# A hybrid convolution and attention block: sums of token quarters split where they are formed

## The chip, the cores and the metric

The kernel runs on one core of a Trainium2 chip. The metric is the time of one execution on the device in microseconds, as the median of several runs. TensorE (PE) does the matmuls, VectorE (DVE), ScalarE (ACT) and GpSimd (POOL) the elementwise work; transfers are issued from the queue of SyncE (SP) and, for some stores, from that of ACT, and run on 16 DMA engines.

## The reference, cut to what matters

A single decoder layer over 2048 tokens of width 1024. All matrices are float32.

```
h = rms_norm(x, norm_w) * (1 + scale) + shift
z = h @ w_in
a, b, g_conv, q, k, v, g_attn, m_conv, m_attn = split(z)
u = silu(layer_norm(causal_conv31(a * sigmoid(b)))) * silu(g_conv)
y_conv = u @ w_conv_out
o = merge of three groups of dilated window attention over rope(rms_norm(q)), rope(rms_norm(k)), v
y_attn = (o * silu(g_attn)) @ w_attn_out
y = sigmoid(m_conv) * y_conv + sigmoid(m_attn) * y_attn
out = x + gate * (y @ w_out)
```

The change concerns `h` on its way into the products with those columns of `w_in` that do not belong to q, k and v.

## The kernel before, in words

**Float32 products out of two parts.** A float32 matrix X is written as an upper part h, X rounded to TensorE's fp32r format, and a lower part l = X - h, also in fp32r. A product takes three matmuls per piece: upper with upper, upper with lower, lower with upper. Making the two parts is called a split here: ACT copies X into h (`nc.scalar.activation(h, raw, AF.Copy)`) and DVE or POOL subtracts (`l = raw - h`). Weights are split as they arrive from memory, activations as they are made.

**First stage: q, k, v and attention.** There are 12 units (three groups of four heads), numbered 0 to 11. A unit goes through 16 steps, one for each block of 128 tokens (`NB`). In a step PE does 24 matmuls of 384 columns (`z_tokens`, L549), and parts of the attention of earlier blocks run between them (`attend_step`), at matmul 5 (flow `beside`) and matmul 14 (flow `main`). After the matmuls ACT and DVE empty the PSUM bank, norm and rotate (`project_step`: squares on ACT L572, their inverse root on POOL L114 and L115, then DVE L586 and L593 to L596). Other small jobs are hung into the steps by `at_step(u, j, m, f)`: f is issued in step j of unit u, before matmul m.

**The matrix h stays in SBUF as quarters.** `hi` and `lo` hold h transposed, in eight tiles each, for half the channels (kh = 0, 1) and 512 tokens (t = 0 to 3). A copy of h in float32 is in memory (`h_d`).

**Second stage: the remaining columns by Strassen's scheme.** The tokens are taken in two halves of 1024. For each half and each pair of 128-column blocks, seven products replace eight (`quad`, L1091). In words of `PRODUCTS`, the left factors are in order A11, A12, S2, S1, S3, S4, A22. Three of them (A11, A12, A22) are quarters of h, the four others are sums and differences of quarters. A product is 12 matmuls of 512 columns. There are 22 jobs (one `quad` each) per half, of kinds `ab_quad` (feeds the convolution), `gate_quad` and `ag_quad`. A slot is one product; slots follow one another in the list `slots`; the last two jobs of the first half and the first two of the second half are interleaved, product by product. Inside a job, ACT copies intermediate sums out of PSUM (`kept`, L1097), DVE adds (L1104, L1118), POOL adds (L1115), and gates are applied on ACT (L1217) and stored. Weights are loaded nine slots ahead (L1039, L1041), combined (L1046) and split seven slots ahead (L1054 on ACT, L1055 on DVE or POOL). DVE runs the convolution in small pieces between all that (`run_conv`), so many per slot.

**How the sums come about before the change.** In units 3 to 7 quarters of h are fetched from `h_d` (`quarter_fetch`, L849) into three tiles of 512 columns, DVE forms the four sums (`quarter_sum`, L853), and each is stored in float32 in `s_d` (L854). This is done eight times (two halves, four channel blocks), 9 steps apart.

**How they land.** *First passage* (from the attention to the first half): in the last unit, whose token blocks are visited in the order 3, 4, ..., 15, 0, 1, 2, the quarters of h that are not needed any more are replaced. From its step 6 on S1, from its step 10 on S2 and S3 are loaded in pieces of 256 columns into a tile `raw`, and one step later ACT and DVE split them into the quarter (`quarter_load` L889, `quarter_split` L895 and L896). S4 is loaded in four pieces of 512 columns into four of the ten buffers of the weights' tile (`wr`) and split in the first four slots. *Second passage* (from the first half to the second): as the interleaved jobs finish product n, its left factor of the first half is given up, and that of the second half is loaded into landing tiles, two pieces per slot, and split two slots later, on ACT and on DVE (for the fourth channel block on POOL). This holds for all seven left factors.

**What sets the order.** The order on PE is the order in the program (`manual_schedule`). On the other engines a planner orders the instructions by a simulated timeline, except for those under `tc.keep_in_program_order`, which keep their place. A queue runs its instructions in order, SP's and ACT's DMA issues among them, and one that waits holds up what is behind it.

The lines that the change and the prediction touch: L849, L853, L854 (forming and storing), L883 to L899 (landing), L902 to L905 (the plan of the first passage), L914 to L925 (the last unit), L1000 and L1001, L1311 to L1325 (S4), L1346 to L1354 (second passage). In the profile the landing tiles are called `rawS`, `s` (S4) and `landingS` or `landingA`; the quarters `S_hi`, `S_lo`, `A_hi`, `A_lo`.

Of the kernel before, what the change touches and what calls it, by code (L numbers as in the profile page):

```python
# [10 lines left out]
F32 = mybir.dt.float32  # L11
F32R = mybir.dt.float32r
# [42 lines left out]
def tile_hybrid_block(  # L55
# [36 lines left out]
    s_d = dram.tile([2, 4, 4, P, 512], F32, name="s_d")  # L92
# [753 lines left out]
    def quarter_fetch(half, k, names):  # L846
        for name, i, kh, t in names:
            q = aside["sq", name] = aside["sq"].tile([P, 512], F32, tag=f"sx{i}", name=f"sx{half}_{k}_{name}")
            nc.sync.dma_start(q, h_d[4 * kh + k, :, 1024 * half + 512 * t : 1024 * half + 512 * t + 512])  # L849

    def quarter_sum(half, k, n, dst, x0, x1, op):
        q = [aside["sq", name] for name in (dst, x0, x1)]
        tc.keep_in_program_order(nc.vector.tensor_tensor(*q, op=op))  # L853
        nc.sync.dma_start(s_d[half, n - 1, k], q[0])  # L854
# [6 lines left out]
    for i in range(8):  # L861
        half, k = divmod(i, 4)
        at = NB * 3 + 8 + 9 * i
        for n, f in ((0, lambda half=half, k=k: quarter_fetch(half, k, (("21", 0, 0, 1), ("22", 1, 1, 1), ("11", 2, 0, 0)))),
                     (1, lambda half=half, k=k: quarter_sum(half, k, 1, "22", "21", "22", ALU.add)),
                     (2, lambda half=half, k=k: quarter_sum(half, k, 3, "21", "11", "21", ALU.subtract)),
                     (4, lambda half=half, k=k: quarter_sum(half, k, 2, "11", "22", "11", ALU.subtract)),
                     (5, lambda half=half, k=k: quarter_fetch(half, k, (("12", 1, 1, 0),))),
                     (7, lambda half=half, k=k: quarter_sum(half, k, 4, "12", "12", "11", ALU.subtract))):
            at_step((at + n) // NB, (at + n) % NB, 23, f)  # L870
# [11 lines left out]
    def quarter_src(half, name, k):  # L882
        if name[0] == "S":  # L883
            return s_d[half, int(name[1]) - 1, k]
        kh, t = {"A11": (0, 0), "A12": (1, 0), "A22": (1, 1)}[name]
        return h_d[4 * kh + k, :, 1024 * half + 512 * t : 1024 * half + 512 * t + 512]
# [4 lines left out]
    def quarter_split(half, name, k, cols, raw, eng):  # L891
# [5 lines left out]
        if half == 0 and name == "S4":  # L897
            tc.keep_in_program_order(i1)
            tc.keep_in_program_order(i2)  # L899
# [870 lines left out]
```

## Time and profile before

| | |
|---|---|
| median of 3 runs | 2373.52 us |
| lowest, highest | 2368.76, 2375.06 us |
| span of the profiled execution | 2368.3 us |
| mean granted clock of TensorE | 0.997 |
| PE busy | 2325.8 us (98%) |
| DVE busy | 1737.0 us (73%) |
| ACT busy | 1020.9 us (43%) |
| POOL busy | 836.1 us (35%) |
| moved by DMA | 378.57 MB, mean 160 GB/s |

The span goes from the first to the last instruction of one profiled execution; the profile does not give that execution's own time beside it. Times on the time axis are microseconds from the start of the span. In a row of the timeline stand start, duration, engine, line of the program, operation, output and inputs, shapes, count, and in brackets the idle time before it and what ended that. In a row of waits stand who waited for whom, the sum, the number and the longest. On the time axis, the attention stage ends near 1076, the second stage begins there, its second half begins near 1513, and the last stages (the projections of both branches, the merge and the output projection) begin near 1930.

### The profile page before, as it was taken

The numbers are of one execution on the slowest core, as the hardware profiler recorded it, in microseconds if no ns is written. First come the engines' busy times: TensorE is split into PE (matmuls) and PEld (weight loads), VectorE is DVE, ScalarE is ACT, GpSimd is POOL, SyncE is SP. The second block draws the span as 40 slices with busy tenths as digits, with TensorE's granted clock in tenths as the row PEclk, the third lists the DMA queues.
The fourth block names the chain that finished last, engine by engine and source line by source line (L and its number), as shares of the span: only waits on it lengthen the run. The fifth ranks groups of instructions, "written<-read, shape, count | busy, mean of one in ns | idle before, by whom it ended". The sixth has DMA issues, their size and how long they took to land.

```text
span 2368.3 us, 38785 instructions
## 1 busy us (share of the span) xinstructions
PE 2325.8 (98%) x12421; PEld 2083.0 (88%) x12421; DVE 1737.0 (73%) x4104; ACT 1020.9 (43%) x2825; POOL 836.1 (35%) x976
## 2 busy tenths in 40 slices
PE   6999999999999999999999999999999999999999
PEld 4899999999999999997888888788888888878887
DVE  7855655555556777776699999989968768787654
ACT  5733343343344555456444444544444444332221
POOL 4321111111111111123677778656556730000221
PEclk9999999999999999999999999999999999999999
DMA  7733544454552222144535445745444569876552
GB/s 279 241 116 117 160 125 144 149 169 149 158 162 67 60 80 67 47 123 154 170 135 176 160 152 195 241 130 151 139 150 134 165 213 330 292 236 204 185 167 102
DMA packets 354121, 378.57 MB, mean 160 GB/s; under 512 B 27688, under 2 KB 249176, under 8 KB 353918
## 3 DMA queue, kind: packets, MB, share of 16 engines
q1 hardware_dynamic: 312622, 314.05, 42.6%
q10 hardware_dynamic: 41296, 62.05, 7.5%
q8 instruction: 99, 1.62, 0.3%
q14 instruction: 104, 0.85, 0.1%
HBM read 235.34 MB, written 140.64 MB: 159 GB/s over the span
## 4 chain that ended last, share of the span: by engine, by line
PE 88%; DMA 4%; DVE 4%; ACT 2%; issue 1%; POOL 1%; SPq 0%; ACTq 0%; DVEq 0%; POOLq 0%
PE pz L549 31%; PE paab L1091 7%; PE yc L1399 6%; PE oa L1681 4%; PE pcab L1091 4%; PE pag_mc_d L1091 4%; PE pag_g_d L1091 3%; PE pag_ma_d L1091 3%; PE po L684 3%; PE ps L635 3%; PE ya L1399 2%; PE pcg_g_d L1091 2%; PE oc L1681 2%; PE pbab L1091 2%; PE paag L1091 2%; PE pcg_mc_d L1091 2%
## 5 line engine op out<-in xcount | busy, mean ns | idle before, releaser
L549 PE MATMUL pz<-wh_u,hT_lo 128*128 128x384 f32 x1504 | 525.2, 349 | 2.5 <-DVE hT_lo L371 2.4
L549 PE MATMUL pz<-wh_u,hT_hi 128*128 128x384 f32 x1504 | 505.6, 336 | 1.3 <-ACT hT_hi L369 1.3
L549 PE MATMUL pz<-wl_u,hT_hi 128*128 128x384 f32 x1504 | 505.8, 336 | 0.0
L114 POOL TENSOR_SCALAR st<-st 128x2 f32<-128x2 f32 x192 | 44.9, 234 | 797.0 <-ACT sq L572 796.7
L586 DVE SCALAR_TENSOR_TENSOR qk<-pz,st,wqk 128x128 f32<-128x128 f32 x384 | 116.9, 346 | 265.0 <-POOL st L115 260.8
L549 PEld LDWEIGHTS pz<-wh_u,hT_lo 128*128 128x128 f32 x1504 | 283.2, 188 | 4.0 <-DVE hT_lo L371 3.7
L549 PEld LDWEIGHTS pz<-wh_u,hT_hi 128*128 128x128 f32 x1504 | 283.8, 189 | 2.2 <-ACT hT_hi L369 1.9
L549 PEld LDWEIGHTS pz<-wl_u,hT_hi 128*128 128x128 f32 x1504 | 282.8, 188 | 0.5 <-issue 0.5
L627 ACT ACTIVATE qkT<-ptq 128x256 f32<-128x256 f32 x192 | 73.8, 384 | 358.1 <-PE ptq L620 302.5
L1169 DVE SCALAR_TENSOR_TENSOR ce<-us,pair_taps,ce 128x512 f32<-128x512 f32 x240 | 180.9, 754 | 6.5
L1140 DVE SCALAR_TENSOR_TENSOR ce<-ut,chan,ce 128x512 f32<-128x512 f32 x240 | 179.8, 749 | 0.0
L1055 POOL TENSOR_TENSOR slT<-wT,shT 128x512 fp32r<-128x512 f32 x107 | 143.8, 1345 | 79.8 <-ACT shT L1054 79.5
L1153 DVE SCALAR_TENSOR_TENSOR cq<-ut,chan,cq 128x512 f32<-128x512 f32 x208 | 156.0, 750 | 1.0
L1054 ACT ACTIVATE shB<-wB 128x512 fp32r<-128x512 f32 x130 | 82.1, 631 | 161.7 <-PE paab L1091 51.7
L115 POOL TENSOR_TENSOR st<-st,mhalf 128x2 f32<-128x2 f32 x192 | 140.1, 729 | 15.9
L572 ACT ACTIVATE sq<-pz 128x128 bf16<-128x128 f32 x384 | 106.1, 276 | 78.7 <-PE pz L549 68.9
L1054 ACT ACTIVATE shT<-wT 128x512 fp32r<-128x512 f32 x110 | 69.4, 631 | 160.9 <-POOL wT L1046 32.0
L1055 POOL TENSOR_TENSOR slB<-wB,shB 128x512 fp32r<-128x512 f32 x85 | 111.9, 1317 | 76.1 <-ACT shB L1054 73.8
L684 PE MATMUL po<-lv,pT 128*128 128x128 f32 x596 | 96.8, 274 | 0.0
L684 PEld LDWEIGHTS po<-lv,pT 128*128 128x128 f32 x596 | 90.9, 190 | 0.6 <-issue 0.5
L593 DVE TENSOR_TENSOR t<-qk,tab 128x256 f32<-128x256 f32 x192 | 82.5, 430 | 5.7
L1055 POOL TENSOR_TENSOR slT<-wB,shT 128x512 fp32r<-128x512 f32 x57 | 75.1, 1324 | 28.4 <-ACT shT L1054 28.3
(783 smaller groups left out, 6163.2 us busy)
## 6 DMA issues: line engine op xcount, KB each, us to landing
wB<-in_w_in_dram SPq DMA_DIRECT2D x154, 256.0 KB, 3.2
qkv_d<-qkv SPq DMA_DIRECT2D x128, 192.0 KB, 2.3
wT<-tT_d SPq DMA_DIRECT2D x88, 256.0 KB, 2.7
tT_d<-wB ACTq DMA_DIRECT2D x66, 256.0 KB, 2.7
lqk<-qkv_d SPq DMA_DIRECT2D x128, 128.0 KB, 2.3
raw_u<-in_w_in_dram SPq DMA_DIRECT2D x84, 192.0 KB, 3.6
acc_d<-osb SPq DMA_DIRECT2D x128, 65.0 KB, 2.0
part<-acc_d ACTq DMA_DIRECT2D x64, 130.0 KB, 2.4
```

Source lines behind the costliest of these rows:

```text
L115: nc.gpsimd.tensor_tensor(dst, scratch[:, :n], mhalf[:, :n], op=ALU.pow)
L549: nc.tensor.matmul(pz[:, :width], part(a, k, P * j, P), w[:, :width], start=(m == 0), stop=(m == 23))
L586: nc.vector.scalar_tensor_tensor(qk[:, 2 * i : 2 * i + 2].rearrange("p a b -> p (a b)"), pz[:, P * i : P * i + P], st[:, 2 + i : 3 + i], w ...
L684: nc.tensor.matmul(po[:, :P], box["pT"][:, P * i : P * i + P], vt, start=(i == 0), stop=(i == nk - 1))
L1054: nc.scalar.activation(h, q[name], AF.Copy)
L1055: eng.tensor_tensor(l, q[name], h.bitcast(F32), op=ALU.subtract)
L1091: nc.tensor.matmul(ps, w, x, start=(m == 0 and ps.name not in first), stop=(m == 11 and not more), skip_group_check=True)
L1140: stt(box["e"], e[:, 1 + j : 513 + j], chan[:, cb, 2 * j : 2 * j + 1], box["e"], op0=ALU.mult, op1=ALU.add)
L1153: stt(box["o"], o[:, 2 + j : 514 + j], w, psum_o, op0=ALU.mult, op1=ALU.add)
L1169: stt(dst, box["both"][:, 1 + j : 513 + j], pair_taps[:, cb, j : j + 1], box["e"], op0=ALU.mult, op1=ALU.subtract if j == 0 else ALU.add)
L1399: nc.tensor.matmul(pz, w, xx, start=(m == 0), stop=(m == len(terms) - 1))
L1681: nc.tensor.matmul(ps, y, w, start=(m == 0 and ps.name not in begun), stop=(m == 11 and not more), skip_group_check=True)
```

## The change

The sums are split where they are formed, and both parts are stored in `s_d`, which becomes twice as large. Forming goes in 16 rounds of 256 columns instead of 8 of 512, 4.5 steps apart instead of 9. In a round four quarters are fetched into four tiles of 256 columns, and from a step and a half later on, at four successive half steps (before matmuls 10 and 23), one sum each is formed: DVE adds, ACT copies the upper part, DVE subtracts for the lower part, all three pinned to the program's order, and SP stores both parts. The parts share three buffers (`sxs`).

At both passages the parts are loaded straight into the quarter's two tiles (`sum_land`), two transfers of 512 columns for each channel block, with no landing tile, copy or subtraction. The load itself now waits until the quarter's old content is done with. The quarters A11, A12 and A22 of the second half land and are split as before. At the first passage S1 is loaded from step 6 of the last unit, S2 and S3 from its step 10, three blocks in two steps; S4 is loaded ahead of the first slots and no longer uses the weights' buffers. At the second passage the loads stand where those of the landing tiles stood.

```
-    s_d = dram.tile([2, 4, 4, P, 512], F32, name="s_d")
+    s_d = dram.tile([2, 2, 4, 4, P, 512], F32, name="s_d")
...
+    def quarter_fetch(half, k, c):
+        for name, kh, t in (("21", 0, 1), ("22", 1, 1), ("11", 0, 0), ("12", 1, 0)):
+            q = aside["sq", name] = aside["sq"].tile([P, 256], F32, tag=f"sx{name}", name=f"sx{half}_{k}_{c}_{name}")
+            t0 = 1024 * half + 512 * t + c
+            nc.sync.dma_start(q, h_d[4 * kh + k, :, t0 : t0 + 256])
+
+    def quarter_sum(half, k, c, n, dst, x0, x1, op):
         q = [aside["sq", name] for name in (dst, x0, x1)]
+        h, l = (aside["sq"].tile([P, 256], F32R, tag="sxs", name=f"sx{hl}{half}_{k}_{c}_{n}", bufs=3) for hl in "hl")
         tc.keep_in_program_order(nc.vector.tensor_tensor(*q, op=op))
-        nc.sync.dma_start(s_d[half, n - 1, k], q[0])
+        tc.keep_in_program_order(nc.scalar.activation(h, q[0], AF.Copy))
+        tc.keep_in_program_order(nc.vector.tensor_tensor(l, q[0], h.bitcast(F32), op=ALU.subtract))
+        for i, x in enumerate((h, l)):
+            nc.sync.dma_start(s_d[i, half, n - 1, k, :, c : c + 256], x.bitcast(F32))
...
+    for i in range(16):
+        half, k, c = i // 8, i // 2 % 4, 256 * (i % 2)
+        at = 2 * (NB * 3 + 8) + 9 * i
+        for n, f in ((0, lambda half=half, k=k, c=c: quarter_fetch(half, k, c)),
+                     (3, lambda half=half, k=k, c=c: quarter_sum(half, k, c, 1, "22", "21", "22", ALU.add)),
+                     (4, lambda half=half, k=k, c=c: quarter_sum(half, k, c, 3, "21", "11", "21", ALU.subtract)),
+                     (5, lambda half=half, k=k, c=c: quarter_sum(half, k, c, 2, "11", "22", "11", ALU.subtract)),
+                     (6, lambda half=half, k=k, c=c: quarter_sum(half, k, c, 4, "12", "12", "11", ALU.subtract))):
+            at_step((at + n) // 2 // NB, (at + n) // 2 % NB, (10, 23)[(at + n) % 2], f)
...
+    def sum_land(half, name, k):
+        if k == 0:
+            quarter_new(half, name)
+        for i in range(2):
+            nc.sync.dma_start(quarters[name][i][:, k].bitcast(F32), s_d[i, half, int(name[1]) - 1, k])
...
                 if last_unit:
-                    for name, k, c0 in placing.pop(p, ()):
-                        raw = wp.tile([P, 384], F32, tag="raw", name=f"raw{name}_{k}_{c0}", bufs=3)[:, :256]
-                        landed.append((0, name, k, slice(c0, c0 + 256), raw))
-                        quarter_load(*landed[-1])
+                    for name, k in placing.pop(p, ()):
+                        sum_land(0, name, k)
...
-    s4 = []
     for k in range(4):
-        s4.append((0, "S4", k, slice(0, 512), wide_raw(f"s4_{k}")))
-        quarter_load(*s4[-1])
+        sum_land(0, "S4", k)
...
-        if s4:
-            quarter_split(*s4.pop(0), nc.vector)
...
         for name, k in asked[:2]:
+            if name[0] == "S":
+                sum_land(1, name, k)
+                continue
             raw = gpa.tile([P, 512], F32, tag="ai" if k == 3 else "gt", name=f"landing{name}_{k}", bufs=2 if k == 3 else 4)
```

More of the change, by code (lines that the diff above doesn't have):

```diff
@@ L896, in quarter_split @@
         i2 = eng.tensor_tensor(l, raw, h.bitcast(F32), op=ALU.subtract)
-        if half == 0 and name == "S4":
-            tc.keep_in_program_order(i1)
-            tc.keep_in_program_order(i2)
+    def sum_land(half, name, k):
[3 more added lines that the diff above has]
+            nc.sync.dma_start(quarters[name][i][:, k].bitcast(F32), s_d[i, half, int(name[1]) - 1, k])
     placing = {}
     for at, names in ((6, ("S1",)), (10, ("S2", "S3"))):
-        for i, piece in enumerate((n, k, c) for k in range(4) for n in names for c in (0, 256)):
-            placing.setdefault(at + i // 3, []).append(piece)
-    landed = []
+        for i, piece in enumerate((n, k) for k in range(4) for n in names):
+            placing.setdefault(at + 2 * i // 3, []).append(piece)
     apart, fetched = {}, [0]
```

22 lines of the change are left out of this document (removed).

## The prediction

> **What bounds the kernel now.** I read the page first, then the list of who waited for whom, restricted to TensorE (PE), then the busy times by stage, then the timelines around the few places where PE waits.
>
> ```profile
> span 2368.3 us, 38785 instructions
> PE 2325.8 (98%) x12421; PEld 2083.0 (88%) x12421; DVE 1737.0 (73%) x4104; ACT 1020.9 (43%) x2825; POOL 836.1 (35%) x976
> ```
>
> PE is busy for all but 42.5 us of the span. The change touches no matmul, so whatever it gains has to come out of those 42.5 us. The list of PE's waits, restricted to 1070 to 1130, the first passage, says who ends them there:
>
> ```profile
> PE ptq L620 <- DVE lqk L596: 2.2, 1, 2.2
> PE ptq L620 <- DVE pT L654: 1.8, 1, 1.8
> PE pcg_g_d L1091 <- DVE osb L686: 1.4, 1, 1.4
> ```
>
> By stage (columns: PE, weight loads, DVE, ACT, POOL busy, then granted clock, DMA share, GB/s):
>
> ```profile
> 320.00:720.00 400.00, 399.65 (x2535) 398.45 (x2534) 229.97 (x850) 157.85 (x660) 73.01 (x157) 1.00 0.51 152
> 1000.00:1070.00 70.00, 70.00 (x462) 69.81 (x461) 53.70 (x212) 38.70 (x151) 15.09 (x38) 1.00 0.39 120
> 1070.00:1126.00 56.00, 50.59 (x262) 42.97 (x261) 38.12 (x110) 37.58 (x86) 17.28 (x20) 1.00 0.47 152
> 1470.00:1526.00 56.00, 51.88 (x222) 42.49 (x221) 54.79 (x72) 35.58 (x67) 40.83 (x30) 0.97 0.76 239
> 1490.00:1495.00 5.00, 5.00 (x24) 4.14 (x23) 5.00 (x8) 2.61 (x5) 3.35 (x3) 1.00 0.96 310
> ```
>
> The reader should see three things. Where the sums are formed (320 to 720) PE has no idle time to speak of (0.35 us), and DVE and ACT have 170 and 242 us free. In the last unit of attention (1000 to 1070) PE is full as well, so work removed there buys nothing. PE loses time in two short stretches only: 5.4 us at the first passage, and 4.1 us at the second one, where DVE is busy for 54.8 of 56 us and the granted clock dips as well.
>
> **The second passage.** First PE, then DVE and ACT:
>
> ```profile
> 1500.34 0.39 PE L1091 MATMUL pcg_ma_d<-S_hi,slB 128*128 128x512 f32 x1
> ...
> 1508.50 0.39 PE L1091 MATMUL pag_ma_d<-hT_hi,slT 128*128 128x512 f32 x1
> 1513.01 0.79 PE L1091 MATMUL paab<-A_hi,shB 128*128 128x512 f32 x1 [4.12 <-ACT spare_hi L1217]
> ...
> 1517.40 0.39 PE L1091 MATMUL pag_g_d<-A_hi,shB 128*128 128x512 f32 x1
> ```
>
> ```profile
> 1506.90 1.72 DVE L896 TENSOR_TENSOR S_lo<-landingS,S_hi 128x512 fp32r<-128x512 f32 x1
> 1508.54 0.67 DVE L1118 TENSOR_TENSOR spare_hi<-spare_hi,pcg_ma_d 128x512 f32<-128x512 f32 x1
> ```
>
> ```profile
> 1509.25 0.63 ACT L1217 ACTIVATE spare_hi<-spare_hi 128x512 f32<-128x512 f32 x1 [3.47 <-DVE spare_hi L1118]
> ...
> 1510.31 1.65 ACT L895 ACTIVATE S_hi<-landingS 128x512 fp32r<-128x512 f32 x3
> ...
> 1512.39 0.57 ACT L1217 ACTIVATE spare_hi<-pag_ma_d 128x512 f32<-128x512 f32 x1
> ```
>
> A product is 12 matmuls. The first two rows are the last matmuls of two products that lie three apart, so one takes (1508.50 - 1500.34) / 3 = 2.72 us, 0.23 per matmul. The next one should have started at 1508.73 and was over at 1517.40: 8.67 us for 2.72, so this place costs **5.95 us**, 4.28 of waiting and 1.67 in which the matmuls come at the dipped clock. The wait is traced back like this. PE wants the bank that ACT empties at 1512.39. ACT had been held at 1509.25 by DVE's addition of 1508.54, and between the two it ran three S copies (1.65 us). DVE's addition could have run when its product ended, soon after 1500.34 + 0.39 = 1500.7; it was 7.8 us late, because DVE was working through S and A subtractions. What these cost stands in the rows of the two lines of the split:
>
> ```profile
> L895 ACT ACTIVATE S_hi<-rawS x24: 401/418/421, 1012.1 to 1051.8; 128x256 fp32r<-128x256 f32 x24
> L895 ACT ACTIVATE S_hi<-landingS x16: 612/623/634, 1488.2 to 1512.9; 128x512 fp32r<-128x512 f32 x16
> ```
>
> ```profile
> L896 DVE TENSOR_TENSOR S_lo<-rawS,S_hi x24: 415/421/427, 1012.6 to 1053.3; 128x256 fp32r<-128x256 f32 x24
> L896 DVE TENSOR_TENSOR S_lo<-landingS,S_hi x12: 675/1114/1726, 1492.0 to 1515.1; 128x512 fp32r<-128x512 f32 x12
> ...
> L896 POOL TENSOR_TENSOR S_lo<-landingS,S_hi x4: 1273/1522/1752, 1490.2 to 1512.0; 128x512 fp32r<-128x512 f32 x4
> ```
>
> The change takes away, from 1488 to 1515, 16 ACT copies (16 x 0.62 = 10 us), 12 DVE subtractions (12 x 1.11 = 13 us) and 4 on POOL (6 us). Eight of the twelve on DVE lie before 1508.54 (the first at 1492.0, the last at 1506.90), some 8 x 1.1 = 9 us; that is more than the 7.8 us by which the addition was late. So the addition comes on time, ACT is not held, its three copies are gone, and the bank is empty when the product before the stall ends. The A quarters keep their splits; they alone did not stall PE (none of its waits lies between 1470 and 1508). Term: **-5.95 us**, bounds 0 (DVE stays late) and -5.95 (there is no more to lose there).
>
> **The first passage.** Its three waits add up to the 5.4 us above. Only one has an S split in front of it:
>
> ```profile
> 1082.97 0.69 DVE L896 TENSOR_TENSOR S_lo<-s,S_hi 128x512 fp32r<-128x512 f32 x1
> ...
> 1086.66 1.77 DVE L896 TENSOR_TENSOR S_lo<-s,S_hi 128x512 fp32r<-128x512 f32 x1
> 1088.36 1.49 DVE L593 TENSOR_TENSOR t<-qk,tab 128x256 f32<-128x256 f32 x1
> ```
>
> DVE is busy without a gap from here to the write of lqk that ends PE's 2.2 us wait. The two subtractions are 2.4 us of that, so at best the whole 2.2 us go. But the 1.77 and the 1.49 are stretched operations (undisturbed, such a subtraction takes 0.68 and a form of 256 columns 0.42), and the stretching has its cause in POOL, which stays: it will fall on the next DVE operations. I take off 0.8 us for it, between nothing and the 1.1 that either of the two is stretched by, and get 2.4 - 0.8: **-1.6 us**; bounds 0 and -2.2. The 1.8 us wait (pT, late behind weight splits) and the 1.4 us wait (osb) have no S split ahead of them, and stay. The landing of S4 now waits on SP for its place in SBUF, and the weight loads of the second job are queued behind it; that place is free once the last unit has left those tokens, three steps of some 5 us before its end, and S4 is only the sixth of the first job's products, at 2.72 us each, so I give it nothing.
>
> **The last unit.** 24 copies (24 x 0.42 = 10 us of ACT) and 24 subtractions (10 us of DVE) go. PE is full in that window: 0. The landings wait on SP for the same tokens as the copies did on ACT.
>
> **Where the sums are formed.** This is what is added. Rows of now:
>
> ```profile
> L853 DVE TENSOR_TENSOR sx<-sx,sx x32: 683/687/691, 347.0 to 700.0; 128x512 f32<-128x512 f32 x32
> ```
>
> ```profile
> 504.61 0.61 DVE L586 SCALAR_TENSOR_TENSOR qk<-pz,st,wqk 128x128 f32<-128x128 f32 x2 [2.30 <-POOL st L115]
> ...
> 507.41 0.68 DVE L853 TENSOR_TENSOR sx<-sx,sx 128x512 f32<-128x512 f32 x1
> ...
> 509.57 0.61 DVE L586 SCALAR_TENSOR_TENSOR qk<-pz,st,wqk 128x128 f32<-128x128 f32 x2 [1.48 <-POOL st L115]
> ```
>
> 32 additions of 512 columns (22 us) become 64 of 256 (64 x 0.42 = 27 us), and 64 ACT copies (27 us) and 64 subtractions (27 us) join them: DVE +32 us of 170 free, ACT +27 of 242 free. SP issues 64 loads instead of 32 and 128 stores instead of 32, all of 128 KB, and the bytes stored double, 8.4 MB more over the 353 us from 347 to 700, 24 GB/s onto 152. All are pinned in program order: ACT waits for the addition, then DVE for ACT's copy, and behind them are queued DVE's evacuations and softmax steps and ACT's qkT and exp. A step lasts 509.57 - 504.61 = 4.96 us; DVE idles 1.48 us in one that has an old addition, so 2.16 us without it. Two sums in a step need 4 x 0.42 = 1.7 us, and two waits for the copy of 0.42 each make it 2.5: 0.35 us over, in 24 of the 72 steps (one or two steps in each round of 4.5 hold two sums). PE uses what DVE makes there one step later, so being late by 0.35 us should be covered; without that cover it would be 24 x 0.35 = 8 us. I take **+0.4 us**, near the 0.35 us of idle time that the stage shows now, with bounds -0.35 (there is no more idle time to lose) and +8.
>
> One rule speaks against this part. The Trainium skill, page "SBUF — State Buffer", section "Who interferes with whom", says that a DVE instruction with two SBUF inputs contends with a GpSimd instruction that reads SBUF. By it the 64 new subtractions and the 64 additions may each be held up beside POOL's per-step work; with the 1.0 us of the stretched 1.72 on each, a step with two sums would be over by some 4 us more and the third rival below would come due. In the trace the 32 additions, two SBUF inputs each, stay within 683 to 691 ns in this stage, so by the row the price is nothing here and the sum is left as it is.
>
> **The sum.** -5.95 - 1.6 + 0.4 = -7.15 us against the profiled execution: span 2368.3 to about 2361.2. The page gives no time of that execution beside its span; the median of the three runs is 2373.52, 5.2 us above the span, and I keep that distance: 2373.5 - 7.1 = **2366.4 us**. About 0.3% (7.1 us) is what a measurement of this kernel can tell from no change, so the forecast lies on that bound.
>
> **The rivals.**
>
> *The transfers take the place of DVE* (chance 0.14). The S landings of the second passage double to 32 of 256 KB, 4.2 MB more, into a stretch whose transfers already run at 0.96 share and 310 GB/s: 13.5 us more of all engines. The A22 loads queue behind them, and ACT stands at its copy of A22 with PSUM copies queued behind it. For it speaks the 0.96; against it, that the next S quarter is not used until a full pair of jobs later and that weights are loaded several products ahead. If ACT is held some 10 us, the bank copies behind it are late by about 4 us and PE waits that long: -7.15 + 4 = -3, 2370.4 us.
>
> *The passage stays late for another reason* (0.13): DVE is still behind from the A splits, or a new order of the unpinned instructions puts splits ahead of the evacuations. Half of the 5.95 and of the 1.6 remain: -3.4, 2370.1 us. Against it speaks that 9 us of DVE work leave ahead of a 7.8 us delay.
>
> *The pinned chain overruns the attention steps* (slower, 0.10). Place: units 3 to 7; point: when a step with two sums is late by more than PE's one step of cover, or when ACT's wait for the addition pushes qkT and exp past their use. Then each of the 24 full steps costs PE the 0.84 us of the two waits: 20 us, net +13, 2386.5 us. For it: the 0.35 us shortfall above; against it: the idle time of ACT and DVE in the stage, and PE's 0.35 us of waits in 400.
>
> *More goes than I count* (0.15): with DVE and ACT lighter, the other two waits of the first passage go too: another 3.8 us, 2362.6 us.
>
> **Chances and range.** The forecast has 0.48. Its own spread is about 1.5 us each way, so a little over half of it is past the bound: 0.27; with the last rival that is 0.42 faster. Within the bound are the rest of the forecast (0.21), most of the two middle rivals (0.25): 0.46. Slower: 0.12, the chain's 0.10 and 0.02 of the transfers' worst end. The range runs from all waits at both passages gone with a little of run-to-run scatter (2361) to the middle rivals with the unknown cost of the stage of the sums (2375.5); the chain's case is left out, and a tail on either side.
>
> **What the profile after would show.** Right: PE's wait for ACT L1217 near 1509 gone and the granted clock at 1.00 from 1470 to 1526; DVE in that window clearly under 45 of 56 us; the wait for lqk at the first passage under 1 us; from 320 to 720 PE still above 399 of 400 us, DVE near 262 and ACT near 185. Wrong: PE waits for pT, sm or pz in units 3 to 7; a wait of the S or A22 copies or of a weight split for a DMA that PE then repeats; a DMA share near 1.0 for 30 us and more after 1487.

## The result, and the profile after

The changed kernel takes **2380.14 us** (median of 6 runs, 2378.47 to 2385.07) against 2372.76 us for the kernel before in the same session (6 runs, 2368.40 to 2375.06). The ratio, taken over all runs (the quotient of the two medians is 1.0031), is 1.0039, interval 1.0027 to 1.005: slower by less than half a per cent, where 2366.4 was predicted. The profiled execution took 2378.47 us and has a span of 2376.6 us, 8.3 us more than the span before.

The page's first lines and the list of PE's waits between 1440 and 1545:

```profile
span 2376.6 us, 39172 instructions
PE 2327.4 (98%) x12421; PEld 2083.3 (88%) x12421; DVE 1744.0 (73%) x4160; ACT 1014.7 (43%) x2845; POOL 826.5 (35%) x972
```

```profile
PE paab L1088 <- ACT spare_hi L1214: 9.4, 1, 9.4
PE pag_g_d L1088 <- ACT spare_hi L1094: 1.5, 1, 1.5
PE paab L1088 <- ACT spare_hi L1094: 1.0, 1, 1.0
```

L1088 is the matmul that was L1091, L1214 the gate activation that was L1217, L1094 the `kept` copy. The wait that was to go has more than doubled. By stage, with the columns as before:

```profile
320.00:720.00 400.00, 398.34 (x2518) 395.89 (x2518) 253.33 (x937) 170.00 (x721) 72.71 (x156) 1.00 0.57 173
1000.00:1070.00 70.00, 70.00 (x458) 69.84 (x457) 48.13 (x192) 32.00 (x131) 13.45 (x36) 1.00 0.51 167
1070.00:1126.00 56.00, 52.33 (x276) 44.55 (x275) 37.09 (x111) 34.75 (x82) 18.38 (x23) 1.00 0.46 151
1470.00:1526.00 56.00, 46.60 (x197) 38.09 (x196) 44.36 (x63) 25.88 (x47) 31.10 (x26) 0.91 0.85 285
```

PE is busier at the first passage (52.33 of 56 us; before 50.59), but at the second one it is busy for 46.60 us instead of 51.88, and the clock is 0.91. DVE and ACT lost the work that the prediction took from them there (44.36 and 25.88 us; before 54.79 and 35.58). They are free, and PE still waits. ACT's timeline shows on what:

```profile
1500.92 0.62 ACT L1214 ACTIVATE spare_lo<-spare_lo 128x512 f32<-128x512 f32 x1
1509.73 0.33 ACTq L1215 DMA_DIRECT2D ma_d<-spare_lo  x1
1510.16 0.63 ACT L1051 ACTIVATE shT<-wT 128x512 fp32r<-128x512 f32 x1 [8.62 <-DMA wB<-in_w_in_dram]
...
1515.71 0.33 ACTq L1215 DMA_DIRECT2D ma_d<-spare_hi  x1
1516.14 0.63 ACT L1051 ACTIVATE shT<-wT 128x512 fp32r<-128x512 f32 x1 [4.30 <-DMA S_hi<-s_d]
...
1518.72 0.33 ACTq L1215 DMA_DIRECT2D ma_d<-spare_hi  x1
1519.15 0.63 ACT L1051 ACTIVATE shT<-wT 128x512 fp32r<-128x512 f32 x1 [1.86 <-DMA S_hi<-s_d]
1519.69 0.58 ACT L1214 ACTIVATE spare_hi<-pag_ma_d 128x512 f32<-128x512 f32 x1
```

The activation that makes `spare_lo` ends at 1501.54. Its store is issued by ACT's own queue only at 1509.73, 8.2 us later, and nothing behind it can run. The two other long holes end in the same way. (For the first hole the trace names a weight load as what ended it; the listing below names the load that it was.) The activation of 1519.69 empties the bank that PE has been waiting for since about 1511. In the kernel before, a store followed its activation at once at the same place:

```profile
1505.14 0.63 ACT L1217 ACTIVATE spare_lo<-spare_lo 128x512 f32<-128x512 f32 x1 [0.38 <-POOL spare_lo L1115]
1505.81 0.33 ACTq L1218 DMA_DIRECT2D ma_d<-spare_lo  x1
```

The chain of work that ended last, in order of time, says the same for the changed kernel:

```profile
1507.14 5.33 DMA wT<-tT_d
...
1512.49 6.16 DMA S_hi<-s_d
...
1518.67 0.02 ACTq L1215
...
1519.69 0.59 ACT spare_hi L1214
...
1520.32 5.02 PE paab L1088 x12
```

A *store* of a gate waits for a *load* of a sum's part, to which it has no relation of data. The load in turn was issued, on SP, only when a weight load had landed. The compiled program tells why. Every transfer from SP's and ACT's queues signals one of eight completion counters, taken in turn over both queues, and an issue waits until the transfer that had its counter before has landed. This is the listing of waits for the first of these stores and for the load ahead of it (queue, line, output and input, waits; DMAHW1 is a counter):

```
SP   L904  DMA S1_hi<-s_d      [waits DMAHW1]
ACT  L1215 DMA ma_d<-spare_lo  [waits DMAHW1, Activation]
```

The load is SP's seventh of S1, issued at 1503.21; the store is issued 6.5 us after it. The loads take nearly that long. From issue to landing it was 3.4 us for the S quarters of the second passage before, and is over 5 us now (columns: KB each, median us; the rows of the changed kernel are those of 1485 to 1525). The trace shows few landings, and a median is one of those: a single one of the 16 before, and five of the 32 now, from 4.8 to 6.2 us.

```profile
landingS<-s_d SPq DMA_DIRECT2D x16, 256.0 KB, 3.4
```

```profile
S_hi<-s_d SPq DMA_DIRECT2D x16, 256.0 KB, 5.5
S_lo<-s_d SPq DMA_DIRECT2D x16, 256.0 KB, 5.1
```

The second loss lies where the sums are formed. There PE waits little by itself (1.7 us in three places, each for `qk` of DVE), but DVE stands at the subtraction of the lower part (L857). DVE's waits there between 320 and 720:

```profile
DVE sxl L857 <- DMA s_d<-sxh: 30.2, 19, 3.5
DVE sxl L857 <- ACT sxh L856: 5.6, 12, 0.7
```

The upper and lower parts of a sum come out of three buffers, so the lower part of one sum takes a buffer whose store, of the sum before, must have landed. That costs DVE 30.2 us in 19 places, and as these instructions are pinned, what is behind them in the program waits too. This is not the whole loss. Of PE's 1.7 us, 1.1 come at one spot after the last sum, by another chain: POOL stands 5.5 us at L660 for a load that ACT's queue issues (it issues some loads besides the stores), the inverse root of the step (L115) is behind it, and DVE's `qk` behind that:

```profile
711.26 0.19 POOL L660 COPY stm<-part 128x4 f32<-128x4 f32 x1 [5.51 <-DMA part<-acc_d]
```

```profile
712.60 0.61 DVE L586 SCALAR_TENSOR_TENSOR qk<-pz,st,wqk 128x128 f32<-128x128 f32 x2 [4.17 <-POOL st L115]
```

```profile
713.36 0.41 PE L549 MATMUL pz<-wh_u,hT_hi 128*128 128x384 f32 x1 [1.11 <-DVE qk L586]
```

Set against the kernel before, PE loses 1.3 us at this spot.

To see what each stage does, the start of the same group of matmuls is subtracted in two PE timelines, that of a run and that of the kernel before, at the two ends of a stage. The ends are, in the kernel before: 300.12 and 719.61 (forming), 1069.08 and 1124.73 (first passage), 1470.65 and 1531.02 (second passage), 1900.94 and 2121.65 (the last stages up to the products with `yc`). For the changed kernel the differences are +2.94, -1.31, +8.93 and -1.97 us; the forecast had +0.4, -1.6, -5.95 and nothing. Profiles of kernels that form the sums in the same way differ in the first of these figures, from 2.94 to 5.93.

### The profile page after: what moved, and what is told of

Its sections match the earlier page's. It is cut to its first block, busy times and chain, and to the rows that moved or that the text cites. A ratio compares the mean times of both kernels' runs of the same rounds, so it can differ in the third digit from the quotient of the medians.

```text
span 2376.6 us, 39172 instructions
## 1 busy us (share of the span) xinstructions
PE 2327.4 (98%) x12421; PEld 2083.3 (88%) x12421; DVE 1744.0 (73%) x4160; ACT 1014.7 (43%) x2845; POOL 826.5 (35%) x972
## 4 chain that ended last, share of the span: by engine, by line
PE 63%; DMA 3%; DVE 2%; issue 1%; ACT 1%; POOL 0%; ACTq 0%; SPq 0%; DVEq 0%; POOLq 0%
PE pz L549 10%; PE paab L1088 7%; PE yc L1395 6%; PE pcab L1088 4%; PE pag_mc_d L1088 4%; PE oa L1677 4%; PE pag_g_d L1088 3%; PE pag_ma_d L1088 3%; PE ya L1395 2%; PE oc L1677 2%; PE pbab L1088 2%; PE paag L1088 2%; PE pcg_mc_d L1088 2%; PE pcg_g_d L1088 2%; PE pcg_ma_d L1088 1%; PE po L684 1%
## 5 line engine op out<-in xcount | busy, mean ns | idle before, releaser
L1166 DVE SCALAR_TENSOR_TENSOR ce<-us,pair_taps,ce 128x512 f32<-128x512 f32 x240 | 180.9, 754 | 6.5
L115 POOL TENSOR_TENSOR st<-st,mhalf 128x2 f32<-128x2 f32 x192 | 140.3, 731 | 15.9
L647 ACT ACTIVATE sm<-sm,osb 128x128 f32<-128x128 f32 (+1 forms) x128 | 56.7, 443 | 114.6 <-DVE osb L645 107.6
```

The lines of the kernel that those rows point to most:

```text
L115: nc.gpsimd.tensor_tensor(dst, scratch[:, :n], mhalf[:, :n], op=ALU.pow)
L1166: stt(dst, box["both"][:, 1 + j : 513 + j], pair_taps[:, cb, j : j + 1], box["e"], op0=ALU.mult, op1=ALU.subtract if j == 0 else ALU.add)
```

## The experiments

Each time is the median of 5 to 12 runs, each ratio is against the kernel before in the same session (medians from 2372.11 to 2372.86). The right-hand columns are the stage differences just described, in us, from the profiled execution of each run.

| run | time | ratio and interval | forming | first | second | last |
|---|---|---|---|---|---|---|
| the change | 2380.14 | 1.0039 (1.0027 to 1.005) | +2.94 | -1.31 | +8.93 | -1.97 |
| e1_form | 2377.09 | 1.0015 (1.0006 to 1.0024) | +4.24 | +1.46 | +0.72 | -2.17 |
| e2_first | 2371.28 | 0.9990 (0.9982 to 0.9999) | +0.97 | -0.98 | +1.65 | +1.38 |
| e3_second | 2383.64 | 1.0039 (1.0025 to 1.0053) | +2.24 | +0.23 | +7.96 | +3.45 |
| e4_store_sp | 2376.38 | 1.0016 (1.0006 to 1.0025) | +4.56 | -1.29 | +2.40 | +3.50 |
| e5_big | 2379.37 | 1.0036 (1.0022 to 1.0051) | +3.74 | -1.31 | +6.17 | +1.74 |
| e6_upper | 2369.48 | 0.9992 (0.9982 to 1.0002) | +5.26 | -1.30 | -1.96 | +3.08 |
| e7_upper_pieces | 2372.85 | 1.0005 (0.9996 to 1.0014) | +4.10 | -1.30 | -0.63 | -0.15 |
| e8_load_pool | 2369.14 | 0.9989 (0.9980 to 0.9997) | +4.48 | -0.65 | -5.97 | +1.73 |
| e9_store_pool | 2367.73 | 0.9984 (0.9975 to 0.9993) | +5.93 | -1.32 | -4.42 | -2.20 |
| e10_unpinned | 2370.73 | 0.9989 (0.9981 to 0.9998) | +2.91 | -1.31 | -4.41 | +3.49 |
| e11_spread | 2366.64 | 0.9973 (0.9964 to 0.9982) | 0.00 | -1.29 | -4.41 | +2.43 |
| e12_before_pool | 2377.38 | 1.0020 (1.0011 to 1.0029) | -0.01 | +0.09 | +3.89 | +2.50 |

The last stages differ by -2.2 to +3.5 us from one profile to another with no relation to the edits that we can see. We take that for scatter of single executions: it goes for the most part with how far the profiled execution lies from its kernel's median (6.8 us over in e6_upper, 3.1 under in e1_form). No kernel was profiled twice. It is why the middle columns are read from the profiles and the sum from the medians.

**The parts alone.** e1_form forms the sums in the new way and lands them in the old one (from the upper part only). e2_first changes the first half alone, e3_second the second half alone.

```
e1  -            return s_d[half, int(name[1]) - 1, k]
    +            return s_d[0, half, int(name[1]) - 1, k]      # old landing
e2  +        if half == 1:
    +            nc.sync.dma_start(s_d[0, half, n - 1, k, :, c : c + 256], q[0])
    +            return                                        # raw sum, old landing
e3  +        if half == 0:                                      # the same for the other half
```

> Only the forming is new: sums are split and both parts stored in 64 rounds of 256 columns, but both passages land and split as before, reading the upper part alone (the lower part of the sums is left out of the result). The trace of the changed kernel puts PE 2.9 us later at the end of units 3 to 7 than the kernel before. If that is the price of the forming, this kernel is 3 us over before, ratio 1.001, and its second passage keeps the wait of about 4 us. If the 2.9 us are scatter, it is within 1 us of before in that stage.

> New forming and direct landing for the first half alone; the second half's sums are stored unsplit and land and split as before. Both theories of the second passage expect it to be back at its old price (a wait of about 4 us with a dipped clock). Half of the forming's 2.9 us remains, and the first passage keeps its gain of 1 to 2 us: -1 to +1 us beside before, ratio 1.000.

> New forming and direct landing for the second half alone; the first passage lands and splits as before. If the second passage is what lost the time, all of its loss is here: +8.7 us there and half of the forming, together +9 to +11 us, ratio 1.004. If the loss came from the two passages together (ACT and DVE running in another rhythm from the first one on), it is under half of that.

The loss at the second passage comes only with the new landing there: +7.96 in e3_second, +0.72 and +1.65 in the other two. PE's wait for the bank is 4.3 us in e1_form and 4.5 in e2_first, as in the kernel before (4.12), and 8.1 in e3_second. The first passage gains only with its new landing (-0.98 in e2_first and -1.31 in the change; +1.46 and +0.23 in the two that land in the old way). Forming costs 4.24 for all sums and 0.97 and 2.24 for half of them. Alone, the first half's part of the change is at most slightly faster than the kernel before (its interval ends at 0.9999).

**Two theories for the second passage.** A: ACT stands at the issue of its stores behind S loads that had the same counters, and the PSUM copies behind it are late. B: the doubled bytes saturate the transfers, and whatever needs memory is late, wherever it is issued. The first experiment between them moves eight stores to SP's queue.

```
-            nc.scalar.dma_start(dst[cb + col, :, ...], th)
+            (nc.sync if half == 0 and dst is ma_d and cb >= 4 else nc.scalar).dma_start(dst[cb + col, :, ...], th)
```

> The changed kernel with the gate stores of the last two jobs of the first half (the stores to ma_d from those jobs) issued on SP instead of ACT, nothing else. Theory A (ACT is held at the issue of these stores, because an issue waits for the completion of an earlier transfer that shares its completion counter, and that is an S landing): PE's wait of 9.4 us at the second passage falls under 3 us, and the kernel ends 6 to 9 us under the changed one, ratio 0.999 to 1.001 to before. Theory B (the stretch is bound by bytes: ACT waits for weights and landings that come late because twice as much is moved): who issues the stores changes nothing, the wait stays above 7 us and the ratio at 1.004.

The 9.4 us wait is gone and the clock from 1470 to 1526 is 1.00, but another wait comes just behind. It is PE's wait for ACT, which waits to write into a scratch buffer whose store has not landed:

```profile
PE paab L1088 <- ACT spare_hi L1094: 4.0, 1, 4.0
```

```profile
1527.96 0.60 ACT L1094 ACTIVATE spare_hi<-paab 128x512 f32<-128x512 f32 x1 [2.86 <-DMA ma_d<-spare_hi]
```

On SP the stores stand in line behind the S loads that wait for PE to give up a quarter. The time fell by 3.8 us, less than the 6 to 9 that theory A expected, and theory B, which expected no change, is not met either. That ACT is held by its own store issues is shown; whether bytes would still cost something was open. So the stores went to POOL's queue, whose transfers have completion counters of their own in the compiled program:

```
+            (nc.gpsimd if half == 0 and dst is ma_d and cb >= 4 else nc.scalar).dma_start(dst[cb + col, :, ...], th)
```

> The changed kernel, with the eight gate stores of the last two jobs of the first half issued from POOL's queue instead of ACT's; bytes, loads and their order stay. Theory A (ACT stands at its store issues, which share completion counters with the S loads of SP's queue; the PSUM copies behind it are late): POOL's transfers use counters of their own, so the stores wait for nothing but their activation. PE's 9.4 us wait for the PSUM copy at the second passage goes, as it did with the stores on SP, and the 4.0 us wait that appeared there for a scratch buffer does not come, because a store no longer stands behind S loads. The 1470 to 1526 window has a clock of 1.00, the whole kernel gains 10 to 15 us on the changed one: 2365 to 2370. Theory B (the doubled bytes saturate the transfers, and whatever needs memory is late): the S loads take as long as in the changed kernel, the weights or scratch buffers are late instead, at least 4 us of waits stay within 1500 to 1535, 2374 or more.

The list of PE's waits (1440 to 1545), the window of the second passage, and ACT and POOL around the place:

```profile
PE pag_ma_d L1088 <- ACT spare_hi L1094: 1.1, 1, 1.1
PE paab L1088 <- ACT spare_hi L1094: 1.0, 1, 1.0
```

```profile
1470.00:1526.00 56.00, 56.00 (x247) 45.92 (x246) 52.09 (x67) 28.31 (x51) 42.64 (x38) 1.00 0.83 279
```

```profile
1505.09 0.62 ACT L1214 ACTIVATE spare_lo<-spare_lo 128x512 f32<-128x512 f32 x1
1506.79 0.63 ACT L1051 ACTIVATE shT<-wT 128x512 fp32r<-128x512 f32 x1 [1.08 <-issue]
```

```profile
1507.27 0.56 POOL L1215 DMA_DIRECT2D ma_d<-spare_lo  x1
```

PE is busy for all 56 us at a clock of 1.00. The same bytes move at 279 GB/s, and nobody is late by much. The kernel is at 2367.73 us, 12.4 us below the changed one and inside what theory A expected. Theory B expected 2374 or more and falls. The transfers land no sooner than in the changed kernel (6.4 us in the median of the S_hi loads whose landing the trace shows between 1485 and 1525); ACT no longer stands for them. The Trainium skill, page "DMA: Bandwidth & Descriptors", section "Issuing engines are not separate DMA queues", says that transfers run on the same 16 DMA engines whichever engine starts them, and that starting them from several engines saves only the issuing sequencer's time, usually little beside the transfer. The trace agrees with the first (a DMA share of 0.83 against 0.85). The issue by itself is short here too, 0.33 us on ACT; what another queue saved was the wait ahead of the issue, which held a compute engine for 8.2 us at one store.

The counterpart moves the S loads instead, and leaves the stores on ACT:

```
-            nc.sync.dma_start(quarters[name][i][:, k].bitcast(F32), ...)
+            (nc.gpsimd if half else nc.sync).dma_start(quarters[name][i][:, k].bitcast(F32), ...)
```

> The changed kernel, with the S loads of the second passage issued from POOL's queue (the gate stores stay on ACT's, the weights' loads on SP's). Bytes and number are those of the changed kernel. Theory A (ACT stands at stores behind S loads on shared counters): POOL's transfers have counters of their own, so the gate stores wait for older loads and stores of SP and ACT only, and PE's 9.4 us wait goes; what is new is that POOL stands at the loads until PE gives a quarter up, with weight subtractions (L1052) behind it, up to 4 us for PE; 2366 to 2374. Theory B (bytes): at least 4 us of waits for PSUM copies stay, 2376 or more.

ACT still issues the stores, and they follow their activations at once again:

```profile
1507.84 0.63 ACT L1214 ACTIVATE spare_hi<-spare_hi 128x512 f32<-128x512 f32 x1 [1.15 <-DVE spare_hi L1115]
1508.50 0.33 ACTq L1215 DMA_DIRECT2D ma_d<-spare_hi  x1
```

It gives -5.97 us at the second passage, as much as the 5.95 that the prediction had found there, with 0.7 us of waits left, and 2369.14 us, where theory B expected 2376 or more. Of POOL's own lateness PE sees nothing. So neither ACT's issuing nor the bytes cost the passage this by themselves; it is the stores and the loads on shared counters.

**Number against bytes.** In e6_upper and e7_upper_pieces only the upper parts are loaded at the second passage, in 16 transfers of 256 KB or in 32 of 128 KB; in e5_big everything is loaded, in 8 transfers of 1 MB.

```
e6/e7  +        if half:
       +            for c in range(0, 512, PIECE):           # PIECE = 512 or 256
       +                nc.sync.dma_start(quarters[name][0][:, k, c : c + PIECE].bitcast(F32), s_d[0, half, ..., c : c + PIECE])
       +            return
e5     +                    for i in range(2):
       +                        nc.sync.dma_start(quarters[name][i].bitcast(F32), s_d[i, 1, ...].rearrange("k p c -> p k c"))
```

> The changed kernel, but at the second passage only the upper parts of the sums are loaded, in 32 pieces of 128 KB: as many transfers as in the changed kernel, half the bytes (the upper part takes the place of the lower part in the products, so the lower parts of these four sums are left out of the result). Theory A (counters shared by order and number): the store issues of ACT meet the same predecessors, which land in about 3.4 us instead of 6.2; PE's 9.4 us wait shrinks to between 3 and 6 us and doesn't go; 2374 to 2378. Theory B (bytes alone): half the bytes are what the kernel before moved, so nothing is late any more, wait under 1 us, 2366 to 2370, and the same as with 16 pieces of 256 KB within 1 us.

> As the run with 32 pieces of 128 KB, but in 16 pieces of 256 KB: half the number and half the bytes of the changed kernel (the lower parts of the four sums of the second half are left out of the result here too). Theory A: fewer S loads stand among the eight counters, so fewer of ACT's stores have one ahead of them; the wait is shorter than with 32 pieces by 1 us or more, 2368 to 2376. Theory B: as with 32 pieces within 1 us, 2366 to 2370.

> The changed kernel, but at the second passage each part of a sum's quarter comes in one load of 1 MB: 8 loads instead of 32, the same bytes. Theory A: 24 fewer transfers take a counter, so the stores' predecessors change and most of them are weight loads or older stores; the 9.4 us wait becomes shorter by 3 us or more, or moves to the one store that still has a 1 MB load ahead of it; 2368 to 2377. Theory B (bytes alone): as the changed kernel, wait of 8 to 10 us, 2378 to 2382.

With half the bytes PE's wait is 3.4 us in 32 pieces and 2.1 us in 16. Both fit A and are too long for B, which expected less than 1 us. The bytes count, since they set how long the transfer ahead takes to land (4.1 us for a piece of 128 KB, the median of five landings). The number seems to count, by 1.3 us in one profile of each. The times say less: 2372.85 us in 32 pieces lies under A's range and over B's, and 2369.48 in 16 lies in both. e5_big is a miss for A: its time is that of the changed kernel, in B's range of 2378 to 2382. B's one wait of 8 to 10 us isn't there, though. PE's wait for the gates has split in two. The first, of 2.3 us, is behind a store issued at 1514.12, which had a 1 MB load ahead of it on its counter; that load took 12.2 us to land, the one landing of such a load that the trace shows. The second, of 4.0 us, is behind the store of 1523.89, which had a weight load of 256 KB ahead of it, and that one took 14.3 us among the 1 MB loads. ACT in e5_big, and the chain of work that ended last:

```profile
1516.64 0.62 ACT L1051 ACTIVATE shT<-wT 128x512 fp32r<-128x512 f32 x1
1523.89 0.33 ACTq L1215 DMA_DIRECT2D ma_d<-spare_hi  x1
```

```profile
1509.20 14.34 DMA wT<-tT_d
...
1523.56 0.02 ACTq L1215
```

So fewer and larger loads do not help by themselves: what counts is how long the transfer ahead on the counter still runs when the store is due.

**Forming.** Two theories again. C: the price is the wait for one of three buffers, two sums being too close together. D: the price is the pinned work itself. e10_unpinned takes the pins from the copy and the subtraction, e11_spread puts one sum into each step; both are built on e9_store_pool.

```
e10 -        tc.keep_in_program_order(nc.scalar.activation(h, q[0], AF.Copy))
    +        nc.scalar.activation(h, q[0], AF.Copy)             # and the subtraction likewise
e11 -        for n, f in ((0, ... quarter_fetch(half, k, c)),
    -                     (3, ... 1, ...), (4, ... 3, ...), (5, ... 2, ...), (6, ... 4, ...)):
    +        for n, f in ((-1, ... quarter_fetch(half, k, c, 1)),   # "21" and "22"
    +                     (0, ... quarter_fetch(half, k, c, 0)),    # "11" and "12"
    +                     (2, ... 1, ...), (4, ... 3, ...), (6, ... 2, ...), (8, ... 4, ...)):
```

> The kernel with the gate stores on POOL's queue, and the forming spread: one sum per step instead of two (half steps 2, 4, 6, 8 of a round instead of 3, 4, 5, 6), with two of the four quarters fetched a half step earlier. All pins stay. In that kernel DVE stands 34.7 us at the subtraction of the lower part (L857) from 320 to 720 for stores of earlier parts, since h and l of a sum share three buffers, and PE is about 5 us later at 713 than in the kernel before. Theory C (the price of forming is this buffer wait of pinned instructions, two sums being too close for three buffers): the waits of L857 for stores fall below 10 us, the waits of ACT's L647 for DVE from 95 to under 50, PE's waits for qk go, PE is no more than 2 us later at 713 than in the kernel before; 2362 to 2366. Theory D (the price is the work itself, three pinned instructions per sum on engines that cycle tightly): the same work stays, PE stays 4 to 6 us late, 2366 to 2370.

> The kernel with the gate stores on POOL's queue, where the copy and the subtraction of a sum are no longer pinned to the program's order (the addition still is): the planner places them. Theory C (buffer wait): the three buffers still bind; the planner counts no transfer's exact time, so the waits for stores fall only in part, to between 10 and 35 us, and PE is between 2 and 6 us late at 713; 2364 to 2369. Theory D (pinned order): without the pin DVE and ACT do what is ready first, PE is no more than 2 us late at 713, 2362 to 2365.

DVE's waits at L857 and the stage's window in e11_spread:

```profile
DVE sxl L857 <- ACT sxh L856: 19.2, 30, 1.1
```

```profile
320.00:720.00 400.00, 399.73 (x2535) 398.53 (x2533) 257.43 (x943) 175.39 (x726) 73.41 (x157) 1.00 0.57 174
```

The waits for stores are gone from the list, those for ACT's copy have grown from 5.6 to 19.2 us (the same chain, at another place in the step) and cost PE nothing: it is busy for 399.73 of 400 us, and the stage's difference from the kernel before is 0.00. Without the pins the waits for stores stay at 28.3 us and PE is 2.91 us late. D falls: the same work, pinned as before, costs nothing in e11_spread. C's signs in the stage all came (no waits for stores, 17.6 us of ACT's L647 for DVE where it had been 95), but that the three buffers are the whole cause isn't shown. e11_spread also takes the crowding out of a step with two sums, and PE's stop of 1.3 us behind POOL's L660 is gone with it, which was no wait for these buffers; two sums per step with more than three buffers were not run. The times lie a little over C's ranges: 2366.64 for 2362 to 2366, and 2370.73 for 2364 to 2369 without the pins. At 2366.64 us, ratio 0.9973 (0.9964 to 0.9982), e11_spread beats the kernel before and the changed one. The median is 1.1 us below that of e9_store_pool, from another session, and the two intervals overlap; the stage had given 5.9 us, and in the two profiles the last stages gave back 4.6 us of it. Whether that is scatter alone is open.

**The kernel before with its stores on POOL.** Does that step bring the gain without the change?

> The kernel before, with the eight gate stores of the last two jobs of the first half on POOL's queue: does that step alone bring the gain, without the change? Theory A: no. In the kernel before the store followed its activation at once (1484.08, 1484.73); the 4.1 to 4.5 us wait comes from DVE's late addition, and it stays at 3 to 5 us; 2371 to 2375, as before. Rival: the stores were in the way there too; the wait falls under 2 us, 2366 to 2369, and the change would bring nothing at this passage.

It does not: 2377.38 us, and PE's wait for the bank is 7.9 us, more than either theory expected. DVE's addition, the late one of the prediction, is still behind S subtractions. It comes at 1511.08 (before 1508.54), but PE is 2.1 us later in this profile when the passage begins, so only some 0.5 us of that is new. The rest is on ACT: in the new order of the unpinned instructions an S copy stands ahead of the activation that empties PE's bank, and waits 2.7 us for its landing:

```profile
1508.13 1.72 DVE L896 TENSOR_TENSOR S_lo<-landingS,S_hi 128x512 fp32r<-128x512 f32 x1
...
1511.08 0.67 DVE L1118 TENSOR_TENSOR spare_hi<-spare_hi,pcg_ma_d 128x512 f32<-128x512 f32 x1
```

```profile
1517.68 0.63 ACT L895 ACTIVATE S_hi<-landingS 128x512 fp32r<-128x512 f32 x1 [2.66 <-DMA landingS<-s_d]
1518.22 0.58 ACT L1217 ACTIVATE spare_hi<-pag_ma_d 128x512 f32<-128x512 f32 x1
```

The gain at the second passage needs both: splits gone from DVE and ACT, and stores that don't wait behind loads.

## Why the prediction was wrong, step by step

**Second passage, -5.95: the mechanism was right, the step after it was missing.** The additions of L1115 (before L1118) come nearly on time: the first of the pair starts 1.1 us after the end of its product's last matmul, where it was 7.8 us late before, and the S copies left ACT.

```profile
1502.37 0.39 PE L1088 MATMUL pcg_ma_d<-S_hi,slB 128*128 128x512 f32 x1
```

```profile
1503.90 0.68 DVE L1115 TENSOR_TENSOR spare_hi<-spare_hi,pcg_ma_d 128x512 f32<-128x512 f32 x1
```

With the stores or the loads on another queue the passage gives -4.42 or -5.97. The sentence that failed is "So the addition comes on time, ACT is not held". ACT was held, not by DVE but by its own queue: 8.2 us at the first store, and PE waited 9.4 us. The description of the kernel lists ACT's DMA issues among what a queue runs in order, and the prediction counted for none of them what it waits for.

**The rival of the transfers was right in kind and wrong in place and price.** It had ACT held with PSUM copies behind it, but at the copy of A22, for 4 us, at a chance of 0.14. It was at the store's issue, and against the forecast the passage is +8.93 + 5.95 = 14.9 us worse. What spoke against it ("the next S quarter is not used until a full pair of jobs later") looks only at who needs the data. No one needed it; a store of another tensor stood behind it.

**First passage, -1.6: right, -1.31, the sum partly by luck.** The wait for lqk fell from 2.2 to 0.7 us, as forecast. The wait for pT, which was to stay at 1.8, fell too, and two waits for ACT that nobody forecast took 0.8 us back:

```profile
PE ptq L620 <- DVE pT L654: 0.9, 1, 0.9
PE ptq L620 <- DVE lqk L596: 0.7, 1, 0.7
PE pag_g_d L1088 <- ACT spare_lo L1094: 0.6, 1, 0.6
PE pcg_g_d L1088 <- ACT spare_hi L1094: 0.2, 1, 0.2
```

**The last unit, 0:** right; PE is full there, with 70.00 of 70 us.

**Forming, +0.4: wrong in its working, +2.94.** "Two waits for the copy of 0.42 each" were there (5.6 us in all), but the wait for a buffer (30.2 us) was put at nothing, though the diff's `bufs=3` tells of it: two parts per sum, two sums per step, and a store's landing of some 2.5 us between. The stop behind POOL's L660 (1.3 of the 2.94 us) was not counted either. The bound of +8 held (the largest of the eight profiles with this forming shows +5.93). The rule weighed there, from the Trainium skill, page "SBUF — State Buffer", section "Who interferes with whom", was not the cause. The 64 new subtractions, two SBUF inputs each, took 418 to 427 ns in this stage (425 on average), within the 415 to 427 ns of the same form at the old landing:

```profile
L857 DVE TENSOR_TENSOR sxl<-sx,sxh 128x256 fp32r<-128x256 f32 x64 | 27.2, 425 | 42.5 <-DMA s_d<-sxh 30.2 <-ACT sxh L856 5.6 <-ACT qkT L627 3.1
```

What they cost stands in the last column of this row of the groups, the idle time ahead of them.

**The distance of 5.2 us** between a span and the time was a median of other runs minus one execution. Where both are known they lie 1.9 us apart (2378.47 and 2376.6). By that (an estimate) the execution that was profiled before took some 2370.2 us, 3.3 below the median; the forecast took its gain off the median and isn't wrong by it.

**The markers.** One misled. DVE under 45 of 56 us from 1470 to 1526 was met by the changed kernel (44.36), while PE and much behind it stood still. In e9_store_pool, where PE is full, DVE has 52.09 us: convolution pieces took part of the room (those of L1166 9.8 us, 5.3 before), and the A subtractions took longer there (12.0 us, 9.1 before). The clock was the better marker (0.91, then 1.00). Two signs of being wrong came: PE waited for pz in units 3 to 7, and a weight split on ACT waited 8.62 us for a DMA by the trace, with PE's 9.4 us behind it. The stage of the sums gave 398.34 us of PE, under the 399 that it named. And PE does not lose time in two short stretches only: of its 42.5 us of idle time before, 23.6 lie ahead of 320 and 7.3 behind 1930, where the change does nothing.

## What to carry to other kernels

When a change adds or lengthens transfers, look at every transfer that a compute engine issues from its own queue near them: its issue can wait for an unrelated load that had its completion counter before, and the engine then stands. Moving the stores, or the loads, to a queue with counters of its own was worth 12 or 11 us here (2380.14 less 2367.73 or 2369.14), where the change by itself lost 7 (2380.14 less 2372.76). And where the result of a step leaves by a store, count the buffers against the landing time of that store as well as the engines' work.

## What the runs showed of the hardware that was not expected

The landing time of a transfer whose data nobody waited for still set the pace, through the counters: 3.4 us for the one 256 KB load of a sum at the second passage before whose landing the trace shows, 6.16 us for the load on the chain of the changed kernel, 12.2 for one of 1 MB, and 14.3 for a weight load of 256 KB among those. A store's issue took 0.33 us on ACT's queue and 0.56 us on POOL's (rows above), and PE saw nothing of it. The stage ran at 279 GB/s and a DMA share of 0.83 with PE busy without a gap, so a share of that size is not a loss in itself.
